# Gate stage of a streaming encoder: gating ahead of a slab's lo part, sigmoids behind copies, three sums and a row's split moved

## Chip, cores and metric

The kernel runs on one core of one Trainium2 chip. The metric is the device time of one execution in microseconds. Three runs of the kernel before gave 2480.63, 2480.68 and 2480.74; the median is 2480.68.

## What is computed

Two groups of frames (512 new ones and 8 streams of 16, 640 columns in all) pass through two layers that share their weights. A layer has a feed-forward half step, a mixer and a second feed-forward half step. The change is in the mixer. Cut to what matters here, the reference's mixer is:

```python
z = h @ w_in                                  # conv B, C, V, q, k, v and the gates g
g = sigmoid(g + b_gate)
g_conv, g_attn = split(g)                     # 1024 columns each
y_conv = B * causal_conv3(C * V)              # 512 channels
y_attn = band_attention(q, k, v)              # 512 channels
m = g_conv * (y_conv @ w_conv_out) + g_attn * (y_attn @ w_attn_out)
x = x + m @ w_o
```

## The kernel before

**Engines.** TensorE (PE in the profile, PEld for its weight loads) multiplies; VectorE (DVE) and ScalarE (ACT) do the elementwise work; SP and GpSimd (POOL) issue the loads of weights. In the gate stage TensorE, VectorE and ScalarE run their instructions in the order in which the code writes them (`ORDERED`), so an instruction that waits holds up all that stand behind it on its engine.

**Products.** Every fp32 operand is split in a hi part, cast by ScalarE, and a lo part, source minus hi, made by VectorE. A product is three matmuls: hi·hi, hi·lo and lo·hi. `prep` casts a slab's hi part (L361) and puts its lo part on a list; `flush` (L366) issues the lo parts of that list on VectorE. `split` (L233, L234) does the same for an operand of the next projection.

**By seven.** A two-by-two block product is made of seven block products instead of eight, named 11, 21, 22, N6, T5, T7 and T4. Their weights are blocks of the raw weights or sums of blocks. Each two raw slabs (`raw`, loaded by SP) give four slabs of weights: slab 0 for 11 and 21, slab 1 for N6 and T5, slab 2 for T7 and 22, slab 3 for T4 alone. Slab 1 is one sum `s` (L294) and a sum `one` that POOL's two accumulating loads have made a group ahead; slab 2 needs two more sums on VectorE. `following` preps the next slab but one, `ahead` makes the sums (and issues the loads) of the slab after that, `quiet` takes the slab that TensorE uses next.

**Gate stage.** The function `outputs` runs, in each of the two layers, gate pairs 2, 4, 6, 8, 10, 12 and 14 (two rows of 128 gates each, `gate_pair`) and four row groups of the two output projections (`rows`): co0 after pair 4 and co4 after pair 6 (y_conv, rows 0 to 3 and 4 to 7), ao0 after pair 10 and ao4 after pair 14 (y_attn). Each of them is seven blocks of twelve matmuls.

- A gate pair's blocks stand in the order 11, 21, N6, T5, T7, 22, T4. 11, N6, T7 and T4 add up in one accumulator `pa` (qa). T4 may start only when VectorE has read `pa` after T7 (L1563: g = pa + c5), since T4 adds on to it.
- A row group's blocks stand in the order 11, T5, N6, 21, T7, 22, T4 (`mul`, L1676). 11, N6, T7 and T4 add up in accumulator A (raco, raao), 21 is in B (rbco, rbao), T5 and 22 in c (rcco, rcao). ScalarE copies A after 11 (into B, or into s1 in group co0, L1692) and after N6 (into s2, rs_0, L1703); VectorE adds A after T7 to s5 (rs_1, L1716 through L294). T7 waits for the copy at L1703, T4 for the sum s5.
- `gated` multiplies a result into its gate (L1683, L1685): `gated(0, …, t1)` needs block 21, the others later blocks.

Small work is hung in by places: `call("s")`, "f", "a", "b", "c", "d" and "e" run what the caller gives for that place. `some` takes the next job of a list `tasks` (sigmoids, L1355, and ScalarE's copies of gates, L1736), `due` a result's last products, `total` adds an attention row to its conv row (`mm[m] += gates[8+m]`), `given` splits finished rows for the projection w_o. With the two rows of a tile side by side, rows 0 and 1 lie in `mm_0`, rows 2 and 3 in `mm_1`. The projection w_o (`po`) follows the stage; its second accumulator takes the place of the group's A.

Of the kernel before, what the change touches and what calls it, by code (L numbers as in the profile page):

```python
# [185 lines left out]
def two(ps):  # L186
    return ps[:, :, :HT]
# [7 lines left out]
def trunk(ctx: ExitStack, tc: tile.TileContext, xin, wst, small, pbias, samplebias, kcache, vcache, gfin,  # L195
# [24 lines left out]
    def acc(name):  # L220
        return banks["acc"].tile([P, 2, 512], F32, tag="acc", name=name)

    def att(name):
        return banks["att"].tile([P, 512], F32, tag="att", name=name)
# [4 lines left out]
    def tmp(name):  # L229
        return tp.tile([P, UW], F32, tag="t", name=name)[:, :T]  # L230
# [62 lines left out]
    def add(out, a, b, op=ALU.add):  # L293
        DVE.tensor_tensor(out=out, in0=a, in1=b, op=op)  # L294
# [69 lines left out]
    def flush(n=None):  # L364
        for lo, src, hi in pending[:n]:
            DVE.tensor_tensor(out=lo, in0=src, in1=hi.bitcast(F32), op=ALU.subtract)  # L366
        del pending[:n]
# [16 lines left out]
    def following(last_first=False):  # L384

        prep(len(ready), last_first)

    def ahead():

        source(len(ready))  # L390
# [5 lines left out]
    def quiet():  # L396

        used[0] += 1
        return ready[used[0] - 1]
# [83 lines left out]
    for k in range(KT):  # L483
# [4 lines left out]
        if k % 2 == 0:  # L488
            c = slice(k * P, (k + 2) * P)
# [1008 lines left out]
    def outputs(l, gp, X, st, cs, ycp, yas, sigmoid, gates):  # L1498


        rr, t1, t2 = st.rr, slice(0, HT), slice(HT, T)
# [28 lines left out]
        def gate_pair(m, at={}, rows_next=False):  # L1530
            n = f"{l}_{m}"
            pa, pb, pc = (att(f"q{i}{n}")[:, :HT] for i in "abc")

            def call(place):
                for f in at.get(place, ()):
                    f()

            s0 = quiet()
            ahead()
            call("s")  # L1540
            block(pa, s0, 0, X11, every, True, True)
            ACT.copy(c1, pa)
            following()
            call("f")
            flush()
            u, g = gates[m], gates[m + 1] = [mm[m + i] if m in (2, 6) else tmp(f"g{n}_{i}") for i in range(2)]
            block(pb, s0, 1, X21, every, True, True)
            add(u[:, t1], pb, c1)
            s1 = quiet()
            following()  # L1550
            flush()
            call("a")
            block(pa, s1, 0, XN6, every, False, True)
            ACT.copy(u2, pa)
            call("b")
            block(pc, s1, 1, XT5, every, True, True)
            ACT.copy(c5, pc)
            call("c")
            s2 = quiet()
            following()  # L1560
            ahead()
            block(pa, s2, 0, XT7, every, False, True)
            add(g[:, t2], pa, c5)  # L1563
            DVE.tensor_tensor(out=g[:, t2], in0=g[:, t2], in1=rr[:, t2], op=ALU.mult)
            flush()
            call("d")
            block(pc, s2, 1, X22, every, False, True)
            add(u[:, t2], pc, u2)
            s3 = quiet()
            following(rows_next)  # L1570
            if rows_next:
                flush(1)
            block(pa, s3, 0, XT4, every, False, True)
            DVE.tensor_tensor(out=g[:, t1], in0=pa, in1=rr[:, t1], op=ALU.mult)
            flush()
            off.append(lambda: DVE.tensor_tensor(out=u, in0=u, in1=rr, op=ALU.mult))
            tasks.extend((lambda: sigmoid(u, m), lambda: sigmoid(g, m + 1, -1.0)))
            call("e")
# [74 lines left out]
        def rows(y, ms, at={}, put_off=0):  # L1653

            n = f"{y.name}{l}_{ms[0]}"
            co = y.name == "co"
            gs = [gates[m + (0 if co else KT)] for m in ms]
            B, A = (acc(f"r{i}{n}") for i in "ba")
            a, b = ([z[:, u, :HT] for u in range(2)] for z in (A, B))
            c = [att(f"rc{n}_{u}")[:, :HT] for u in range(2)]  # L1660
            s1, s2, s5 = stage
            seed = seeded[0]
            seeded[0] = True

            def call(place):
                for f in at.get(place, ()):
                    f()

            def mul(ps, s, half, k, start):
                for u in range(2):  # L1670
                    for i in range(2):
                        kp = half * NP + 2 * u + i
                        wh, wl = (z[:, kp * P : (kp + 1) * P] for z in s)
                        xh, xl = y.kind(i, k)
                        for j, (w, x_) in enumerate(((wh, xh), (wh, xl), (wl, xh))):
                            PE.matmul(ps[u], w, x_, start=start and i == 0 and j == 0,  # L1676
                                      stop=i == 1 and j == 2, skip_group_check=True)

            def gated(r, src, t, scale=None):
                for u in range(2):  # L1680
                    g = gs[2 * r + u][:, t]
                    if scale is None:
                        DVE.tensor_tensor(out=g, in0=src[u], in1=g, op=ALU.mult)  # L1683
                    else:
                        DVE.scalar_tensor_tensor(out=g, in0=src[u], scalar=scale, in1=g,  # L1685
                                                 op0=ALU.mult, op1=ALU.mult)

            w = quiet()
            ahead()
            call("s")  # L1690
            mul(a, w, 0, "11", True)
            ACT.copy(two(B) if seed else s1, two(A))  # L1692
            following()
            call("f")
            flush()
            call("a")
            w1 = quiet()
            mul(c, w1, 1, "T5", True)
            for u in range(2):
                ACT.copy(s5[:, u], c[u])  # L1700
            call("b")
            mul(a, w1, 0, "N6", False)
            ACT.copy(s2, two(A))  # L1703
            call("c")
            mul(b, w, 1, "21", not seed)
            following()
            if not seed:
                add(s1, two(B), s1)
            flush()
            w = quiet()  # L1710
            following()
            gated(0, b if seed else [s1[:, u] for u in range(2)], t1)
            ahead()
            call("d")
            mul(a, w, 0, "T7", False)
            add(s5, two(A), s5)  # L1716
            flush()
            left = [lambda: gated(1, [s5[:, u] for u in range(2)], t2, -1.0),
                    lambda: gated(0, [s2[:, u] for u in range(2)], t2), lambda: gated(1, a, t1, -1.0)]

            if not put_off:
                left.pop(0)()
            mul(c, w, 1, "22", False)
            for u in range(2):
                add(s2[:, u], c[u], s2[:, u])
            w = quiet()
            following()
            if not put_off:
                left.pop(0)()
            mul(a, w, 0, "T4", False)  # L1730
            flush()
            while len(left) > put_off:
                left.pop(0)()
            off.extend(left)
            if co:
                tasks.extend(lambda u=u: ACT.copy(mm[ms[u]], gs[u]) for u in range(2))  # L1736
            call("e")
# [3 lines left out]
        def total(*ms):  # L1741
            for m in ms:
                add(mm[m], mm[m], gates[KT + m])

        def begun(*ms):
            for m in ms:
                mo[m] = tuple(hp.tile([P, T], F32R, tag=f"h{i}", name=f"m{l}_{m}{i}") for i in ("hi", "lo"))

        def given(*ms):
            for m in ms:  # L1750
                split(*mo[m], mm[m])

        def quarters(z):
            return z.rearrange("p c (a b) -> p (c a) b", a=2)

        def joined(*zs):
            return {k: [f for z in zs for f in z.get(k, ())] for k in "sfabcde"}

        due_, task = {"f": [due]}, lambda *ks: {k: [some()] for k in ks}
        yc = Mixed("co", [quarters(z) for z in ycp])  # L1760
        ya = Mixed("ao", [quarters(yas[:, 2 * i : 2 * i + 2]) for i in range(2)])
# [7 lines left out]
        gate_pair(8, joined(due_, one, task("b", "d")))  # L1769
        gate_pair(10, joined(due_, two_, task("b")), True)  # L1770
        rows(ya, (0, 1, 2, 3), joined(three, {"a": [due]}, task("b", "c", "d")), 1)
        gate_pair(12, joined({"f": [lambda: total(0)]}, {"a": [lambda: total(1)]}, {"a": [due]},
                             {"a": [lambda: total(2, 3)]}))
        gate_pair(14, joined(due_, task("b", "e"), {"c": [lambda: (begun(*range(4)), given(0, 2))]}), True)
        rows(ya, (4, 5, 6, 7), joined(due_, {"a": [lambda: given(1, 3)]}, task("b", "c")))
        assert not tasks
        begun(*range(4, KT))
        total(4, 5)
# [659 lines left out]
```

## Time and profile before

| | |
|---|---|
| median of three runs | 2480.68 us |
| the profiled execution | 2480.66 us |
| its span, first to last instruction | 2478.8 us |
| mean granted TensorE clock | 0.999 |
| TensorE matmul busy | 2461.0 us (99%) |
| VectorE busy | 2194.8 us (89%) |
| ScalarE busy | 1397.8 us (56%) |
| GpSimd busy | 326.0 us (13%) |
| gate stage of layer 0 | about 634 to 773.5 us from the span's start |
| gate stage of layer 1 | about 1863 to 2002 us |

A row of the timeline gives start and duration in microseconds, engine, line, operation, output and inputs (buffer numbers left out), shapes, a count of equal instructions that were drawn together, and in brackets the idle time of that engine before it with the instruction that ended it. A row of the waits view gives the waiting engine and line, what it waited for, the total, the number of times and the longest. A row of the windows gives the length of the stretch, then for PE, PEld, DVE, ACT and POOL the busy time and the number of instructions, then the granted clock, the share of the DMA engines and GB/s; its row "sum" adds up the stretches. Matmuls overlap: one starts before the one ahead of it has ended.

### The profile page before, as it was taken

Reading aid. Unit: us, or ns where it says so; the run is one execution under the profiler, and the core shown is the slowest. Engines: PE = TensorE matmul, PEld = TensorE weight load, DVE = VectorE, ACT = ScalarE, POOL = GpSimd, SP = SyncE. Lnnn points to the kernel's source line nnn. Section 1 sums busy time; section 2 is a strip of 40 time slices with the busy share of each in tenths; the row PEclk is TensorE's granted clock in tenths of the full one; section 3 lists DMA queues with packets and bytes.
Section 4 is the critical chain, followed back from the end, with each engine's and each line's share of the span. In section 5 each row is a group of like instructions: output and inputs, shape, how many; then the busy total and the mean of one; then the engine's idle time right before and its main releaser. Section 6 shows DMA issues by size and latency. Waiting matters only on the chain.

```text
span 2478.8 us, 44038 instructions
## 1 busy us (share of the span) xinstructions
PE 2461.0 (99%) x17216; PEld 2406.7 (97%) x17216; DVE 2194.8 (89%) x3684; ACT 1397.8 (56%) x2243; POOL 326.0 (13%) x491
## 2 busy tenths in 40 slices
PE   8999999999999999999999999999999999999999
PEld 8999999889999999999999999998899999999998
DVE  7999998888998899998799999988889979999997
ACT  6555555665655555555665555566656556555555
POOL 0211112211110001111001011121110000111111
PEclk9999999999999999999999999999999999999999
DMA  4443444335443334445334343453454333444444
GB/s 155 128 118 102 124 118 121 112 111 175 120 121 120 92 102 107 112 118 121 108 95 109 110 117 102 117 128 105 136 166 120 113 118 94 107 113 107 112 118 117
DMA packets 114417, 290.26 MB, mean 117 GB/s; under 512 B 13120, under 2 KB 52672, under 8 KB 114208
## 3 DMA queue, kind: packets, MB, share of 16 engines
q1 hardware_dynamic: 69552, 220.10, 27.6%
q0 software_dynamic: 44224, 67.09, 14.2%
q8 instruction: 135, 2.21, 0.4%
q14 instruction: 74, 0.61, 0.1%
q10 hardware_dynamic: 432, 0.25, 0.0%
HBM read 241.57 MB, written 7.94 MB: 101 GB/s over the span
## 4 chain that ended last, share of the span: by engine, by line
PE 90%; DVE 5%; ACT 2%; issue 1%; DMA 1%; SPq 0%; DVEq 0%; ACTq 0%; POOLq 0%
PE pab L460 12%; PE paa L460 11%; PE pcb L460 6%; PE daa L1148 6%; PE pca L460 5%; PE dab L1148 5%; PE po L436 5%; PE qa L460 3%; PE pbb L460 3%; PE dca L1148 3%; PE pba L460 3%; PE dcb L1148 2%; PE ma_cv L460 2%; PE ma_qk L460 2%; PE pv L1837 2%; PE qc L460 2%
## 5 line engine op out<-in xcount | busy, mean ns | idle before, releaser
L366 DVE TENSOR_TENSOR wlo<-raw,whi 128x512 fp32r<-128x512 f32 (+1 forms) x566 | 577.7, 1023 | 150.3 <-ACT whi L361 147.1
L361 ACT CAST whi<-raw 128x512 fp32r<-128x512 f32 (+1 forms) x566 | 500.6, 891 | 372.6 <-PE pbb L460 47.3
L361 ACT CAST whi<-s 128x1024 fp32r<-128x1024 f32 (+1 forms) x166 | 155.2, 935 | 288.9 <-issue 111.2
L460 PE MATMUL pab<-xhib,whi 128*128 128x320 f32 x704 | 217.7, 309 | 0.0
L460 PE MATMUL pab<-xlob,whi 128*128 128x320 f32 x704 | 217.2, 309 | 0.0
L460 PE MATMUL pab<-xhib,wlo 128*128 128x320 f32 x704 | 217.2, 309 | 0.0
L460 PE MATMUL paa<-xhia,whi 128*128 128x320 f32 x640 | 197.8, 309 | 0.2 <-DVE ga L294 0.2
L460 PE MATMUL paa<-xhia,wlo 128*128 128x320 f32 x640 | 197.5, 309 | 0.0
L460 PE MATMUL paa<-xloa,whi 128*128 128x320 f32 x640 | 197.5, 309 | 0.0
L366 DVE TENSOR_TENSOR wlo<-s,whi 128x1024 fp32r<-128x1024 f32 (+1 forms) x166 | 179.1, 1079 | 4.0 <-ACT whi L361 4.0
L1170 POOL DMA_DIRECT2D x<-c_a x80 | 69.8, 1018 | 574.8 <-ACT ahia L1052 205.6
L1170 POOL DMA_DIRECT2D x<-c_b x72 | 63.1, 1014 | 583.1 <-ACT ahib L1052 205.9
L460 PEld LDWEIGHTS pab<-xhib,whi 128*128 128x128 f32 x704 | 132.2, 188 | 0.9 <-issue 0.9
L460 PEld LDWEIGHTS pab<-xlob,whi 128*128 128x128 f32 x704 | 132.2, 188 | 0.0
L460 PEld LDWEIGHTS pab<-xhib,wlo 128*128 128x128 f32 x704 | 132.2, 188 | 0.0
L460 PEld LDWEIGHTS paa<-xhia,whi 128*128 128x128 f32 x640 | 120.1, 188 | 1.1 <-DVE ga L294 0.5
L460 PEld LDWEIGHTS paa<-xloa,whi 128*128 128x128 f32 x640 | 120.1, 188 | 0.2 <-DVE xloa L704 0.2
L460 PEld LDWEIGHTS paa<-xhia,wlo 128*128 128x128 f32 x640 | 120.1, 188 | 0.1
L294 DVE TENSOR_TENSOR raw<-s,raw 128x512 f32<-128x512 f32 x166 | 113.6, 684 | 0.0
L460 PE MATMUL pcb<-xhib,wlo 128*128 128x320 f32 x352 | 108.8, 309 | 0.0
L460 PE MATMUL pcb<-xhib,whi 128*128 128x320 f32 x352 | 108.7, 309 | 0.0
L460 PE MATMUL pcb<-xlob,whi 128*128 128x320 f32 x352 | 108.6, 309 | 0.0
(889 smaller groups left out, 8244.2 us busy)
## 6 DMA issues: line engine op xcount, KB each, us to landing
raw<-in_wst SPq DMA_DIRECT2D x375, 512.0 KB, 3.6
x<-c_a POOLq DMA_DIRECT2D x80, 160.0 KB, 4.5
x<-c_b POOLq DMA_DIRECT2D x72, 160.0 KB, 3.5
one<-in_wst POOLq DMA_DIRECT2D x40, 256.0 KB, 3.5
lent<-in_wst POOLq DMA_DIRECT2D x36, 256.0 KB, 3.8
kc<-in_kcache SPq DMA_DIRECT2D x32, 256.0 KB, 5.0
vc<-in_vcache SPq DMA_DIRECT2D x16, 512.0 KB, 4.5
x<-u_a POOLq DMA_DIRECT2D x40, 160.0 KB, 4.1
```

Of the source, the lines that this page charges most:

```text
L294: DVE.tensor_tensor(out=out, in0=a, in1=b, op=op)
L361: ACT.copy(hi[:, d], src[:, c])
L366: DVE.tensor_tensor(out=lo, in0=src, in1=hi.bitcast(F32), op=ALU.subtract)
L436: PE.matmul(ps[:, a, :HT], w, x[a] if isinstance(x, tuple) else x[:, a * HT : (a + 1) * HT], start=first and j == 0 and not seeded, stop=l ...
L460: PE.matmul(ps, a, b, start=start and kp == 0 and j == 0, stop=stop and kp == NP - 1 and j == 2, skip_group_check=True)
L1148: PE.matmul(ps[u], w, y, start=start and i == 0 and j == 0, stop=i == 1 and j == 2, skip_group_check=True)
L1170: POOL.dma_start(x[ms[2 * u + r]][:, cols], z[:, u], accum_op=ALU.add)
L1837: PE.matmul(pv[t], xx[:, t * P : (t + 1) * P], w[:, kk * AW : (kk + 1) * AW], start=c == 0 and kk == 0 and j == 0, stop=c == KT // 2 - 1 a ...
```

## The change

Nothing is added to the computation or taken from it; every engine has as many instructions as before. In `rows`, three moves:

- place "c", where a sigmoid of the task list is issued on ScalarE, goes from ahead of block 21 to behind the cast of slab 3;
- the first gating, `gated(0, …, t1)`, goes ahead of the flush of slab 3's lo part;
- `ahead()`, the sum `s` of the next group with the loads that belong to it, goes behind the sum s5;

On ScalarE, the copy after N6, the cast of slab 3, the sigmoid of place "c", the cast of the next slab and the sigmoid of place "d" now follow each other.

In the list of the groups: the totals of rows 0 and 1 now stand together at place "f" of pair 12 (before: 0 at "f", 1 at "a"); row 2's stays at "a"; row 3's goes to place "a" of pair 14. Row 2's split goes from place "c" of pair 14, where row 0's stays, to place "d", behind the lo part of the next slab. In group ao4 the two sigmoids go from places "b" and "c" to "c" and "d".

```diff
             ACT.copy(s2, two(A))
-            call("c")
             mul(b, w, 1, "21", not seed)
             following()
             if not seed:
                 add(s1, two(B), s1)
+            call("c")
+            gated(0, b if seed else [s1[:, u] for u in range(2)], t1)
             flush()
             w = quiet()
             following()
-            gated(0, b if seed else [s1[:, u] for u in range(2)], t1)
-            ahead()
             call("d")
             mul(a, w, 0, "T7", False)
             add(s5, two(A), s5)
+            ahead()
             flush()
...
-        gate_pair(12, joined({"f": [lambda: total(0)]}, {"a": [lambda: total(1)]}, {"a": [due]},
-                             {"a": [lambda: total(2, 3)]}))
-        gate_pair(14, joined(due_, task("b", "e"), {"c": [lambda: (begun(*range(4)), given(0, 2))]}), True)
-        rows(ya, (4, 5, 6, 7), joined(due_, {"a": [lambda: given(1, 3)]}, task("b", "c")))
+        gate_pair(12, joined({"f": [lambda: total(0, 1)], "a": [due, lambda: total(2)]}))
+        gate_pair(14, joined(due_, {"a": [lambda: total(3)]}, task("b", "e"),
+                             {"c": [lambda: (begun(*range(4)), given(0))], "d": [lambda: given(2)]}), True)
+        rows(ya, (4, 5, 6, 7), joined(due_, {"a": [lambda: given(1, 3)]}, task("c", "d")))
```

## Prediction

> **What bounds the kernel now.** I read the page's head, then TensorE's waits, then the windows of the first layer's gate stage (eight windows, 634.0 to 773.5 us), then the timeline around each wait.
>
> ```profile
> span 2478.8 us, 44038 instructions
> PE 2461.0 (99%) x17216; PEld 2406.7 (97%) x17216; DVE 2194.8 (89%) x3684; ACT 1397.8 (56%) x2243; POOL 326.0 (13%) x491
> ```
> ```profile
> PE raao L1676 <- DVE rs L294: 1.5, 2, 0.8
> ```
> ```profile
> sum 139.50, PE 137.43 PEld 135.96 DVE 127.30 ACT 83.89 POOL 11.42; mean PE 17.18 PEld 17.00 DVE 15.91 ACT 10.49 POOL 1.43
> ```
>
> TensorE is the bound, so an edit counts only by the waits of TensorE that it ends or makes. The waits view has each wait twice, once per layer; I work out one layer and double it. In these windows weight loading stood idle for 139.50 - 135.96 = 3.54 us. The timeline shows where:
>
> ```profile
> 670.01 0.19 PEld L1676 LDWEIGHTS raco<-y4co_0hi,whi 128*128 128x128 f32 x1 [0.46 <-issue]
> ...
> 707.12 0.19 PEld L460 LDWEIGHTS qa<-thi,whi 128*128 128x128 f32 x1 [0.18 <-DVE g L294]
> ...
> 728.33 0.31 PE L1676 MATMUL raao<-y4ao_0hi,whi 128*128 128x320 f32 x1
> ...
> 731.71 0.31 PE L1676 MATMUL rcao<-y2ao_1hi,wlo 128*128 128x320 f32 x1
> ...
> 732.74 0.19 PEld L1676 LDWEIGHTS raao<-y4ao_0hi,whi 128*128 128x128 f32 x1 [0.99 <-ACT whi L361]
> ...
> 732.77 0.39 PE L1676 MATMUL raao<-y4ao_0hi,whi 128*128 128x320 f32 x1 [0.75 <-DVE rs L294]
> ...
> 733.00 0.30 PE L1676 MATMUL raao<-y4ao_0lo,whi 128*128 128x320 f32 x1
> ...
> 746.03 0.19 PEld L460 LDWEIGHTS qa<-thi,whi 128*128 128x128 f32 x1 [0.98 <-DVE g L294]
> ...
> 758.84 0.19 PEld L460 LDWEIGHTS qa<-thi,whi 128*128 128x128 f32 x1 [0.49 <-DVE g L294]
> ...
> 768.05 0.19 PEld L1676 LDWEIGHTS raao<-y4ao_0hi,whi 128*128 128x128 f32 x1 [0.41 <-ACT rs L1703]
> ...
> 777.08 0.30 PEld L436 LDWEIGHTS po<-m_0hi,whi 128*128 128x128 f32 x2 [0.19 <-issue]
> ```
>
> These are, in order: block T4 of group co0, T4 of gate pair 8, T4 of group ao0, T4 of pairs 12 and 14, T7 of group ao4, and the projection's second accumulator. Matmuls follow each other at 0.147 us (728.33 to 731.71 is 23 steps), so a block of twelve takes 1.76. What a wait costs: 731.71 to 733.00 is 1.29 for two steps of 0.147, so 1.00 is lost. That is the weight load's idle time (0.99), not the matmul's 0.75.
>
> [...]
>
> **Row groups: gating ahead of the lo part.** VectorE's queue in group ao0 (g_8 are gates, wlo_8361/8362 the fourth slab's lo part, s_108 a slab sum, rs_1 the sum s5, rbao block 21):
>
> ```order
> -L366 TENSOR_TENSOR wlo_8362<-raw_8237,whi_8361 128x512
>  L1683 TENSOR_TENSOR g_8_0_8041<-rbao_0_8292,g_8_0_8041 128x320
>  L1683 TENSOR_TENSOR g_8_1_8042<-rbao_0_8292,g_8_1_8042 128x320
> -L294 TENSOR_TENSOR s_108_8377<-one_8239,raw_8365 128x512
> +L366 TENSOR_TENSOR wlo_8361<-raw_8237,whi_8360 128x512
>  L294 TENSOR_TENSOR rs_1_7304<-raao_0_8293,rs_1_7304 128x640
> -L366 TENSOR_TENSOR wlo_8368<-raw_8365,whi_8367 128x1024
> +L294 TENSOR_TENSOR s_108_8391<-one_8239,raw_8367 128x512
> +L366 TENSOR_TENSOR wlo_8370<-raw_8367,whi_8369 128x1024
> ```
> The gatings pass the lo part, and the s5 sum, which frees the accumulator for T4, passes the slab sum.
>
> ```profile
> 728.43 0.83 ACT L1355 ACTIVATE g<-g,sm 128x640 f32<-128x640 f32 x1 [0.96 <-DVE g L1576]
> ...
> 729.80 0.69 DVE L366 TENSOR_TENSOR wlo<-raw,whi 128x512 fp32r<-128x512 f32 x1 [1.41 <-ACT whi L361]
> ...
> 731.21 0.68 DVE L294 TENSOR_TENSOR s<-one,raw 128x512 f32<-128x512 f32 x1
> 731.81 0.82 DVE L294 TENSOR_TENSOR rs<-raao,rs 128x640 f32<-128x640 f32 x1
> ```
>
> Ao0: VectorE idled 1.41 for a cast that stood behind the sigmoid of 728.43. Now the cast goes first, and the gatings start when block 21 ends: 728.33 + 0.17 (a matmul lasts 0.31, 0.17 beyond the next one's start) = 728.5. Two gatings take 0.80 and the lo part 0.60 (the row groups' spacing), so VectorE is free at 729.9 and the sum waits only for T7's end, 728.33 + 1.76 + 0.17 = 730.26. It ends at 731.12 instead of 732.63; the load follows 0.11 later (732.63 to 732.74), and was due at 731.75. **0.99 goes**, margin about 0.5.
>
> ```profile
> 665.99 0.31 PE L1676 MATMUL rbco<-y2co_1hi,wlo 128*128 128x320 f32 x1
> ...
> 666.33 0.82 DVE L294 TENSOR_TENSOR capsm<-rbco,capsm 128x640 f32<-128x640 f32 x1
> ...
> 667.68 0.89 DVE L1683 TENSOR_TENSOR g<-capsm,g 128x320 f32<-128x320 f32 x2
> ...
> 669.08 0.82 DVE L294 TENSOR_TENSOR rs<-raco,rs 128x640 f32<-128x640 f32 x1
> ```
>
> Co0: the first add starts 0.03 after block 21's end (666.30), so TensorE's release is prompt. The slab sum (0.60) leaves the way; the gatings now read the add directly, at its end (667.15 + 0.04) where the lo part could start at 667.08: 0.11 back. The sum comes 0.49 earlier. **0.46 goes**, with no margin left.
>
> ```profile
> 692.84 0.31 PE L1676 MATMUL raco<-y4co_1hi,wlo 128*128 128x320 f32 x1
> ...
> 693.63 0.82 DVE L294 TENSOR_TENSOR rs<-raco,rs 128x640 f32<-128x640 f32 x1
> 694.37 1.22 DVE L366 TENSOR_TENSOR wlo<-raw,whi 128x1024 fp32r<-128x1024 f32 x1
> ...
> 706.59 0.48 DVE L294 TENSOR_TENSOR g<-qa,c 128x320 f32<-128x320 f32 x1
> ```
> ```profile
> 698.20:721.20 23.00, 23.00 (x158) 22.82 (x157) 22.83 (x42) 14.48 (x25) 2.54 (x4) 1.00 0.48 138
> ```
>
> Co4, a cost: no wait stood here. T7 ends at 693.15; the slab sum used the time before it, and now follows. Sum at 693.20, slab sum 693.94, next lo part 694.54 instead of 694.37. From there VectorE (third count of the window, 22.83 of 23.00) has no gap to absorb it until the add of 706.59, for which pair 8's T4 waits already: 0.18 becomes 0.35. **0.17 is added.**
>
> The moved step also issues loads, on SP and on POOL:
>
> ```profile
> one<-in_wst POOLq DMA_DIRECT2D x40, 256.0 KB, 3.5
> ```
>
> Both queues keep their order. Two such loads, 7 us, fill one of two buffers, whose use is a group (7 × 1.76 = 12.3 us) further on: nothing. If that cover failed, the slab sum would wait by the difference.
>
> **Gate pair 12.** VectorE's queue (mm += g are the totals):
>
> ```order
>  L294 TENSOR_TENSOR mm_0_7301<-mm_0_7301,g_8_0_8041 128x640
> -L366 TENSOR_TENSOR wlo_8449<-raw_8365,whi_8448 128x1024
> -L294 TENSOR_TENSOR g_12_0_8453<-qb_12_8431,capsm_4819 128x320
> -L366 TENSOR_TENSOR wlo_8469<-raw_8372,whi_8468 128x512
>  L294 TENSOR_TENSOR mm_0_7301<-mm_0_7301,g_8_1_8042 128x640
> +L366 TENSOR_TENSOR wlo_8449<-raw_8367,whi_8448 128x1024
> +L294 TENSOR_TENSOR g_12_0_8454<-qb_12_8431,capsm_4819 128x320
> +L366 TENSOR_TENSOR wlo_8470<-raw_8386,whi_8469 128x512
>  L1685 SCALAR_TENSOR_TENSOR g_10_0_8177<-raao_0_8293,g_10_0_8177 128x320
>  L1685 SCALAR_TENSOR_TENSOR g_10_1_8178<-raao_0_8293,g_10_1_8178 128x320
>  L294 TENSOR_TENSOR mm_1_7302<-mm_1_7302,g_10_0_8177 128x640
> +L294 TENSOR_TENSOR s_110_8512<-one_8388,raw_8502 128x512
> ```
> The second total moves ahead of the lo part, and the fourth leaves for pair 14.
>
> ```profile
> 739.74 1.23 DVE L366 TENSOR_TENSOR wlo<-raw,whi 128x1024 fp32r<-128x1024 f32 x1 [0.44 <-ACT whi L361]
> ...
> 743.42 1.55 DVE L294 TENSOR_TENSOR mm<-mm,g 128x640 f32<-128x640 f32 x2
> 744.89 0.69 DVE L294 TENSOR_TENSOR s<-one,raw 128x512 f32<-128x512 f32 x1
> 745.49 0.49 DVE L294 TENSOR_TENSOR g<-qa,c 128x320 f32<-128x320 f32 x1
> ```
>
> A total takes 0.74 (743.42 to 744.89 for two). VectorE enters the pair 0.91 earlier (the sum 1.51 earlier, the slab sum's 0.60 back). The second total costs 0.74 - 0.44 of idle = 0.30 there, and two totals leave further on: 745.49 becomes 745.49 - 0.91 + 0.30 - 1.48 = 743.40, ending at 743.89. TensorE comes 0.99 earlier and wants T4's weights at 745.05 - 0.99 = 744.06. **0.98 goes**, margin 0.1 to 0.2.
>
> **Gate pair 14.**
>
> ```profile
> 756.22 0.83 DVE L234 TENSOR_TENSOR m_0lo<-mm,m_0hi 128x640 fp32r<-128x640 f32 x1 [1.82 <-ACT m_0hi L233]
> ...
> 758.30 0.48 DVE L294 TENSOR_TENSOR g<-qa,c 128x320 f32<-128x320 f32 x1
> ```
>
> The fourth total fits into the 1.82 of idle time. Row 2's lo part (0.74, as the total) leaves the way of the add at 758.30: **0.49 goes**, margin 0.25.
>
> **Group ao4.** ScalarE's queue (rs_0 is the copy s2, g_14 the sigmoids):
>
> ```order
>  L1700 COPY rs_1_7304<-rcao_4_1_8703 128x320
> -L1355 ACTIVATE g_14_0_8585<-g_14_0_8585,sm 128x640
>  L1703 COPY rs_0_7303<-raao_4_8701 128x640
> -L1355 ACTIVATE g_14_1_8586<-g_14_1_8586,sm 128x640
> -L361 CAST whi_8769<-raw_8648 128x512
> -L361 CAST whi_8775<-raw_8773 128x1024
> -L361 CAST whi_8812<-raw_8780 128x1024
> +L361 CAST whi_8767<-raw_8646 128x512
> +L1355 ACTIVATE g_14_0_8584<-g_14_0_8584,sm 128x640
> +L361 CAST whi_8776<-raw_8774 128x1024
> +L1355 ACTIVATE g_14_1_8585<-g_14_1_8585,sm 128x640
> ```
> The sigmoid ahead of the copy goes behind it and a cast.
>
> ```profile
> 766.58 0.84 ACT L1355 ACTIVATE g<-g,sm 128x640 f32<-128x640 f32 x1
> 767.32 0.68 ACT L1703 COPY rs<-raao 128x640 f32<-128x640 f32 x1
> ...
> 769.27 0.69 DVE L366 TENSOR_TENSOR wlo<-raw,whi 128x512 fp32r<-128x512 f32 x1 [1.75 <-ACT whi L361]
> ```
>
> The copy comes 0.74 earlier (766.58 to 767.32). But its chain hangs on VectorE, which does row 2's lo part ahead of it, so it does not gain pair 14's 0.49: 0.41 - 0.74 + 0.49 = 0.16 stays, **0.25 goes**. The gatings' 0.80 moves into the 1.75 of idle time, so **0.19** goes at the projection.
>
> **Sum.** 0.99 + 0.46 - 0.17 + 0.98 + 0.49 + 0.25 + 0.19 = 3.19 per layer, 6.4 in all. The profiled execution took 2480.66 us (span 2478.8), as the median of 2480.68: 2474.3, with a span of 2472.4. The granted clock is 1.00 in the quoted window (third number from the end): no term.
>
> **Rivals.** Forecast, 2474.3: 0.74. Its own range: if pair 8's wait does not grow and goes too (0.35) and T7's rest goes (0.16), 3.7 per layer, 2473.3; if the three small margins fail by 0.1 and pair 8's by 0.2, 0.5 back, 2475.3.
>
> *VectorE 0.3 later than counted throughout*: back come 0.3 (co0), 0.3 (pair 8), 0.15 (pair 12), 0.05 (pair 14), 0.25 (T7): 2.1 left, 2476.4. For it: zero margin at co0, and 127.30 of 139.50 us busy. Against: the idle times above. 0.14.
>
> *Waits cost only the matmul's idle time*: then 0.24 less comes back at each of the four T4 waits that go (0.99 against 0.75), 2.2 left, 2476.2; 0.04. Against: the 1.29 measured. [...]
>
> *The moved waits only meet the next one*, since VectorE has the same work: 2480.7. Against: the same idle times. 0.04.
>
> *Slower*: the gatings, now first in VectorE's strict order, wait not for block 21 but for T7's end, 1.76 later, with lo part, sums and slab sum queued behind. Then the sum starts 0.42 (co0) and 0.97 (co4) later than before; TensorE loses 0.42 and, with 0.05 of slack (sum and release end at 694.56, the load is due at 692.84 + 12 × 0.147 = 694.60), 0.92; pair 8's T4 0.65 more; ao0 and pair 12 gain only 0.24; pair 14, ao4 and the projection keep 0.93: 0.8 per layer worse, 2482.3. Linear between, the gain is gone from 1.4 us after block 21 on. Against: co0's add, 0.03 after its release. 0.04.
>
> A measurement can tell about 0.2% (5.0 us) from no change. Faster by more means below 2475.7: the forecast, less what falls beyond its range, and a little of the first rival: 0.74. The slower rival stays within 0.2%, so slower by more is 0.02, and same 0.24. The range, 2473.2 to 2476.6, leaves out the last two rivals and some 0.06 of the forecast's ends.
>
> **What would show it.** Right: no idle time on weight loads at T4 of co0, ao0, pairs 12 and 14; 0.3 to 0.4 at pair 8; at most 0.2 at ao4's T7; the ao0 gating within 0.1 of block 21's end. Wrong: weight-load idle time in the stage above 1.5 us per layer, a wait on a lo part, or a slab sum waiting for a load.

## The result, and the profile after

The changed kernel takes 2474.33 us, the median of 11 runs (2473.73 to 2476.59), where the kernel before took 2480.68 in 11 runs beside it (2480.34 to 2481.27). The ratio is 0.9975, with a 95% interval of 0.9966 to 0.9984: 6.35 us less, 0.25%, and the interval leaves out 1. The forecast was 2474.3. The profiled execution took 2474.65 us.

The head of the page of the changed kernel:

```profile
span 2472.9 us, 44032 instructions
PE 2459.8 (99%) x17216; PEld 2408.0 (97%) x17216; DVE 2194.5 (89%) x3684; ACT 1397.2 (57%) x2243; POOL 326.7 (13%) x491
```

The busy times of all engines are within 1.5 us of those before, so no work went. What went is idle time of TensorE. First, the sum of eight windows over the first layer's gate stage (634.0 to 771.0 us) and the weight loads' waits on a sum `g` by the waits view; then, from the weight loads' timeline, the two rows of this stage that still have an idle time (707.33 and 765.55), and among those that have none now T4 of co0, ao0 and pair 12 and the projection's second accumulator:

```profile
sum 137.00, PE 136.93 PEld 136.47 DVE 128.39 ACT 84.17 POOL 11.45; mean PE 17.12 PEld 17.06 DVE 16.05 ACT 10.52 POOL 1.43
```
```profile
PEld qa L460 <- DVE g L294: 0.7, 2, 0.3
```
```profile
670.06 0.19 PEld L1676 LDWEIGHTS raco<-y4co_0hi,whi 128*128 128x128 f32 x1
...
707.33 0.19 PEld L460 LDWEIGHTS qa<-thi,whi 128*128 128x128 f32 x1 [0.34 <-DVE g L294]
...
731.92 0.19 PEld L1676 LDWEIGHTS raao<-y4ao_0hi,whi 128*128 128x128 f32 x1
...
744.22 0.19 PEld L460 LDWEIGHTS qa<-thi,whi 128*128 128x128 f32 x1
...
765.55 0.19 PEld L1676 LDWEIGHTS raao<-y4ao_0hi,whi 128*128 128x128 f32 x1 [0.19 <-ACT rs L1703]
...
774.30 0.34 PEld L436 LDWEIGHTS po<-m_0hi,whi 128*128 128x128 f32 x2
```

Weight loading stood idle for 137.00 - 136.47 = 0.53 us, at T4 of pair 8 and at T7 of group ao4. Before, the seven waits that the prediction lists summed to 0.46 + 0.18 + 0.99 + 0.98 + 0.49 + 0.41 + 0.19 = 3.70. So 3.17 went per layer; the second layer's rows read the same (0.34 and 0.19), which makes 6.34 in both.

The stage's length agrees. The first matmul of pair 2 and the first of the projection, in TensorE's timeline of the kernel before and then of the changed one:

```profile
634.49 0.31 PE L460 MATMUL qa<-hhim,whi 128*128 128x320 f32 x1
...
773.47 0.45 PE L436 MATMUL po<-m_0hi,whi 128*128 128x320 f32 x2
```
```profile
635.01 0.31 PE L460 MATMUL qa<-hhim,whi 128*128 128x320 f32 x1
...
770.93 0.45 PE L436 MATMUL po<-m_0hi,whi 128*128 128x320 f32 x2
```

From 138.98 to 135.92 us, 3.06 less, and the projection's wait on top. This execution came to the stage 0.52 later than the other, in work that the change does not touch, so the two profiled spans differ by only 5.9.

VectorE's timeline of the changed kernel, at the places where the prediction worked out a time: group ao0, then group co0, then group co4 with the add in pair 8, and the add in pair 12.

```profile
728.74 0.89 DVE L1683 TENSOR_TENSOR g<-rbao,g 128x320 f32<-128x320 f32 x2
729.55 0.68 DVE L366 TENSOR_TENSOR wlo<-raw,whi 128x512 fp32r<-128x512 f32 x1
730.50 0.82 DVE L294 TENSOR_TENSOR rs<-raao,rs 128x640 f32<-128x640 f32 x1 [0.27 <-PE raao L1676]
```
```profile
667.71 0.89 DVE L1683 TENSOR_TENSOR g<-capsm,g 128x320 f32<-128x320 f32 x2
668.52 0.68 DVE L366 TENSOR_TENSOR wlo<-raw,whi 128x512 fp32r<-128x512 f32 x1
669.13 0.82 DVE L294 TENSOR_TENSOR rs<-raco,rs 128x640 f32<-128x640 f32 x1
```
```profile
693.23 0.82 DVE L294 TENSOR_TENSOR rs<-raco,rs 128x640 f32<-128x640 f32 x1 [0.27 <-PE raco L1676]
693.98 0.68 DVE L294 TENSOR_TENSOR s<-one,raw 128x512 f32<-128x512 f32 x1
694.58 1.22 DVE L366 TENSOR_TENSOR wlo<-raw,whi 128x1024 fp32r<-128x1024 f32 x1
...
706.80 0.48 DVE L294 TENSOR_TENSOR g<-qa,c 128x320 f32<-128x320 f32 x1
...
743.53 0.48 DVE L294 TENSOR_TENSOR g<-qa,c 128x320 f32<-128x320 f32 x1
```

In ao0 the 1.41 of idle time before the lo part is gone: the lo part follows the gatings, and the sum waits for T7's end, as worked out. In co0 nothing waits any more, but the sum starts at the moment at which VectorE comes free. In co4 the sum waits for T7's end (0.27) and the slab sum follows it, ahead of the lo part: the order that was to cost 0.17 at pair 8. In pair 12 the add ends at 743.53 + 0.48 = 744.01, 0.21 ahead of T4's weight load at 744.22; 743.89 and 744.06, 0.17 apart, were worked out.

In pair 14 VectorE's idle time before row 0's split is 1.08 where it was 1.82: the fourth total fills 0.74 of it.

```profile
752.53 0.82 DVE L294 TENSOR_TENSOR mm<-mm,g 128x640 f32<-128x640 f32 x1
...
754.43 0.83 DVE L234 TENSOR_TENSOR m_0lo<-mm,m_0hi 128x640 fp32r<-128x640 f32 x1 [1.08 <-ACT m_0hi L233]
```

### The profile page after: what moved, and what is told of

Its sections match the earlier page's. It is cut to its first block, busy times and chain, and to the rows that moved or that the text cites. A ratio compares the mean times of both kernels' runs of the same rounds, so it can differ in the third digit from the quotient of the medians.

```text
span 2472.9 us, 44032 instructions
## 1 busy us (share of the span) xinstructions
PE 2459.8 (99%) x17216; PEld 2408.0 (97%) x17216; DVE 2194.5 (89%) x3684; ACT 1397.2 (57%) x2243; POOL 326.7 (13%) x491
## 4 chain that ended last, share of the span: by engine, by line
PE 94%; DVE 3%; ACT 2%; issue 1%; DMA 0%; DVEq 0%; ACTq 0%; POOLq 0%
PE pab L460 12%; PE paa L460 11%; PE pcb L460 6%; PE daa L1148 6%; PE pca L460 5%; PE dab L1148 5%; PE po L436 5%; PE qa L460 4%; PE pbb L460 3%; PE dca L1148 3%; PE pba L460 3%; PE dcb L1148 2%; PE ma_cv L460 2%; PE ma_qk L460 2%; PE pv L1837 2%; PE qc L460 2%
```

## The experiments

Each kernel was run beside the kernel before, which gave medians of 2480.88, 2480.71 and 2481.14 us on the three chips used. All compute the whole reference. Diffs are against the changed kernel; `...` stands for lines that are not shown.

**The row groups alone, and the lists alone.** The first keeps the three moves in `rows` and has the lists of jobs as before; the second is the reverse.

```diff
rows_only:
-        gate_pair(12, joined({"f": [lambda: total(0, 1)], "a": [due, lambda: total(2)]}))
+        gate_pair(12, joined({"f": [lambda: total(0)]}, {"a": [lambda: total(1)]}, {"a": [due]},
+                             {"a": [lambda: total(2, 3)]}))
...
lists_only:
+            call("c")
             mul(b, w, 1, "21", not seed)
...
-            call("c")
-            gated(0, b if seed else [s1[:, u] for u in range(2)], t1)
             flush()
             w = quiet()
             following()
+            gated(0, b if seed else [s1[:, u] for u in range(2)], t1)
+            ahead()
             call("d")
             mul(a, w, 0, "T7", False)
             add(s5, two(A), s5)
-            ahead()
```

> Only the three moves inside the row groups; the totals, row 2's split and group ao4's sigmoids stand as before. My theory (TensorE waits for single instructions of VectorE and ScalarE, and the waits add up one by one): weight loads idle per layer 0 at T4 of co0 and ao0, 0.35 us at pair 8's T4, 1.06 at pair 12's T4 (0.98 plus the 0.08 by which TensorE comes earlier than VectorE), 0.49 at pair 14's T4, 0.41 at ao4's T7, together 2.3 against 3.7 before: 2477.9 us. Rival (the row groups' waits only move on to the pairs, since VectorE has the same work): pair 12 takes back the whole 0.99 and the time stays within 0.5 us of 2480.7.

> Only the moves of the totals, of row 2's split and of ao4's sigmoids; the code inside the row groups stands as before. My theory: the waits of co0 (0.46), pair 8 (0.18) and ao0 (0.99) stay, those of pairs 12 and 14 and of the projection go, 0.16 to 0.2 stays at ao4's T7, together 1.8 per layer: 2476.9 us. Rival (the parts need each other): pair 12 keeps 0.5 or more of its wait without the row group's earlier sum, 2478 or more.

rows_only took 2477.91 us (2477.63 to 2478.98), ratio 0.9988 (0.9979 to 0.9997). The weight loads of its first gate stage:

```profile
706.72 0.19 PEld L460 LDWEIGHTS qa<-thi,whi 128*128 128x128 f32 x1 [0.34 <-DVE g L294]
...
744.72 0.19 PEld L460 LDWEIGHTS qa<-thi,whi 128*128 128x128 f32 x1 [1.07 <-DVE g L294]
...
757.52 0.19 PEld L460 LDWEIGHTS qa<-thi,whi 128*128 128x128 f32 x1 [0.49 <-DVE g L294]
...
766.73 0.19 PEld L1676 LDWEIGHTS raao<-y4ao_0hi,whi 128*128 128x128 f32 x1 [0.40 <-ACT rs L1703]
```

The waits at co0 and ao0 are gone. Pair 12's is 1.07 where it was 0.98, 0.09 more as expected, and pair 14's stays at 0.49, instead of growing by the 0.99 that went at ao0. The rival by which the waits only move on falls here.

lists_only took 2477.80 us (2476.94 to 2478.98), ratio 0.9987 (0.9978 to 0.9995), 0.9 above what was expected. Its weight loads:

```profile
646.01 0.19 PEld L460 LDWEIGHTS qa<-thi,whi 128*128 128x128 f32 x1 [0.25 <-DVE mm L294]
671.11 0.19 PEld L1676 LDWEIGHTS raco<-y4co_0hi,whi 128*128 128x128 f32 x1 [0.46 <-issue]
708.22 0.19 PEld L460 LDWEIGHTS qa<-thi,whi 128*128 128x128 f32 x1 [0.18 <-DVE g L294]
733.83 0.19 PEld L1676 LDWEIGHTS raao<-y4ao_0hi,whi 128*128 128x128 f32 x1 [0.99 <-ACT whi L361]
767.43 0.19 PEld L1676 LDWEIGHTS raao<-y4ao_0hi,whi 128*128 128x128 f32 x1 [0.19 <-ACT rs L1703]
776.46 0.30 PEld L436 LDWEIGHTS po<-m_0hi,whi 128*128 128x128 f32 x2 [0.20 <-issue]
```

Pairs 12 and 14 wait no more, ao4's T7 waits 0.19 instead of 0.41, and co0, pair 8 and ao0 wait as before: the two halves of the change act each at its own places. Of the 0.9 too much, 0.4 is the projection's wait, which I had expected to go with the lists (0.20 in each of two layers); it goes by the moves inside `rows`, made in ao4 too, which this kernel lacks. The first row, at T4 of pair 2, is new and lies ahead of everything that the change touches; it is taken up at the end.

**Which move in the row groups takes ao0's wait.** Three kernels put back the sigmoid's move, the gatings' move, or both; the slab sum stays behind s5 in all.

```diff
sigmoid_back:
             ACT.copy(s2, two(A))
+            call("c")
...
-            call("c")
             gated(0, b if seed else [s1[:, u] for u in range(2)], t1)
...
gating_back:
             call("c")
-            gated(0, b if seed else [s1[:, u] for u in range(2)], t1)
             flush()
             w = quiet()
             following()
+            gated(0, b if seed else [s1[:, u] for u in range(2)], t1)
```

> The changed kernel with place c, the sigmoid, back ahead of block 21, so that the sigmoid stands ahead of slab 3's cast again. My theory: with the gatings ahead of the lo part VectorE has work until the cast comes, the lo part in ao0 ends at most 0.5 us later and the sum s5 waits for T7's end all the same: no wait comes back, 2474.3 us. Rival (the sigmoid behind the copy is what ended ao0's wait): 0.4 us or more of weight-load idle time at ao0's T4, 2475.1 to 2476.3 us.

> The changed kernel with the first gating back behind slab 3's lo part. My theory: the cast now comes ahead of the sigmoid, so that the lo part is done while VectorE would wait for block 21, and the sum s5 starts at T7's end as in the changed kernel: no wait comes back, and co0's margin grows by 0.1: 2474.3 us. Rival (the gating's place is what ended ao0's wait): 0.4 us or more at ao0's T4, 2475.1 to 2476.3 us.

> The changed kernel with both the sigmoid and the gating back in their old places; of the moves inside the row groups only the slab sum's stays. My theory (either of the two moves ends ao0's wait, and without both it stands again, less the slab sum's 0.60): per layer 0.44 us of weight-load idle time at ao0's T4, and 0.41 at pair 12's T4, since VectorE enters the pair as late as before; 0.34 at pair 8 and 0.19 at ao4's T7 as in the changed kernel: 2476.0 us. Rival (the slab sum's move alone did it): 2474.3 us.

sigmoid_back took 2474.17 us (2474.02 to 2474.72) and gating_back 2474.22 (2473.92 to 2475.05), both at a ratio of 0.9972 (0.9961 to 0.9983): no different from the changed kernel. Their weight loads wait 0.35 at pair 8 and 0.20 at ao4's T7, and nowhere else. both_back took 2476.53 us (2475.77 to 2477.20), ratio 0.9982 (0.9974 to 0.9991). Its VectorE in group ao0, its weight loads there and in pair 12, and the matmul of the first of these two loads:

```profile
730.30 0.69 DVE L366 TENSOR_TENSOR wlo<-raw,whi 128x512 fp32r<-128x512 f32 x1 [1.41 <-ACT whi L361]
730.91 0.88 DVE L1683 TENSOR_TENSOR g<-rbao,g 128x320 f32<-128x320 f32 x2
731.71 0.81 DVE L294 TENSOR_TENSOR rs<-raao,rs 128x640 f32<-128x640 f32 x1
```
```profile
732.64 0.19 PEld L1676 LDWEIGHTS raao<-y4ao_0hi,whi 128*128 128x128 f32 x1 [0.39 <-issue]
...
745.26 0.19 PEld L460 LDWEIGHTS qa<-thi,whi 128*128 128x128 f32 x1 [0.29 <-DVE g L294]
```
```profile
732.67 0.39 PE L1676 MATMUL raao<-y4ao_0hi,whi 128*128 128x320 f32 x1 [0.15 <-DVE rs L294]
```

With both put back, the 1.41 of idle time for a cast that stands behind a sigmoid is there again, and 0.39 of ao0's 0.99 (0.44 was expected); the other 0.60 is the slab sum, which still stands behind s5. VectorE enters pair 12 late enough for 0.29 (0.41 was expected), and the projection waits 0.20 again, which was not expected. The median lies 0.5 above the 2476.0 that was. So, with the slab sum behind s5, the rest of ao0's wait goes by either of two moves: put the cast ahead of the sigmoid, or give VectorE the gatings to do in its place. One is redundant beside the other, but not both.

**The slab sum, the row's split, the fourth total: each put back alone.**

```diff
sum_back:
+            ahead()
             call("d")
             mul(a, w, 0, "T7", False)
             add(s5, two(A), s5)
-            ahead()
...
split_back:
-                             {"c": [lambda: (begun(*range(4)), given(0))], "d": [lambda: given(2)]}), True)
+                             {"c": [lambda: (begun(*range(4)), given(0, 2))]}), True)
...
total_back:
-        gate_pair(12, joined({"f": [lambda: total(0, 1)], "a": [due, lambda: total(2)]}))
-        gate_pair(14, joined(due_, {"a": [lambda: total(3)]}, task("b", "e"),
+        gate_pair(12, joined({"f": [lambda: total(0, 1)], "a": [due, lambda: total(2, 3)]}))
+        gate_pair(14, joined(due_, task("b", "e"),
```

> The changed kernel with the slab sum back ahead of the sum s5. My theory: co0's T4 waits again, 0.57 to 0.62 us; ao0's does not, because its sum s5 still ends before the block; pair 8's T4 no longer waits, because the slab sum runs in the time before T7's end: per layer 0.60 back and 0.34 gone, 2474.8 us. Rival (pair 8's wait has another cause than the slab sum): it stays at 0.34, 2475.5 us.

> The changed kernel with row 2's split back beside row 0's in pair 14. My theory: pair 14's T4 waits again, 0.5 us, and ao4's T7 no longer does, since the lo part no longer stands ahead of the slab sums on which ScalarE's copy hangs: per layer 0.52 back and 0.19 gone, 2475.0 us. Rival (T7's rest has another cause): 0.19 stays, 2475.4 us.

> The changed kernel with the fourth total back in pair 12. My theory: pair 12's T4 waits 0.74 less its margin of 0.15, 0.6 us per layer, and nothing else changes: 2475.5 us. Rival (the earlier sum in ao0 alone ended pair 12's wait): no wait, 2474.3 us.

sum_back took 2474.99 us (2474.33 to 2477.34), ratio 0.9977 (0.9968 to 0.9986). VectorE and the weight load at group co0:

```profile
667.83 0.69 DVE L366 TENSOR_TENSOR wlo<-raw,whi 128x512 fp32r<-128x512 f32 x1
668.43 0.69 DVE L294 TENSOR_TENSOR s<-one,raw 128x512 f32<-128x512 f32 x1
669.03 0.82 DVE L294 TENSOR_TENSOR rs<-raco,rs 128x640 f32<-128x640 f32 x1
```
```profile
669.97 0.19 PEld L1676 LDWEIGHTS raco<-y4co_0hi,whi 128*128 128x128 f32 x1 [0.59 <-issue]
```

The slab sum ahead of s5 costs one slab sum (0.60) at co0, and pair 8 does not wait at all: the move is worth 0.59 in one group and costs 0.34 behind another. At ao0 nothing waits here: with the sigmoid and the gatings moved, the slab sum's move is not needed there.

split_back took 2474.74 us (2474.14 to 2475.52), ratio 0.9975 (0.9965 to 0.9984). Pair 14 waits 0.49 again and ao4's T7 not at all, as expected. total_back took 2475.46 us (2475.05 to 2477.55), ratio 0.9979 (0.9970 to 0.9988). Pair 12 waits 0.54 (0.6 was expected). The weight loads of split_back at pair 14 and of total_back at pair 12:

```profile
756.71 0.19 PEld L460 LDWEIGHTS qa<-thi,whi 128*128 128x128 f32 x1 [0.49 <-DVE g L294]
```
```profile
744.79 0.19 PEld L460 LDWEIGHTS qa<-thi,whi 128*128 128x128 f32 x1 [0.54 <-DVE g L294]
```

**No wait left.** The last two waits answer to two of these moves, so both can go: the slab sum stays ahead of s5 in the groups other than co0, and row 2's split is taken apart, its cast at place "d" of pair 14 as in the changed kernel (`high`), its lo part at the head of group ao4's place "a" (`low`). The definitions of these two are not shown. `seed` is false in group co0 and true in the other groups. The changed kernel was run again beside it.

```diff
             following()
+            if seed:
+                ahead()
             call("d")
             mul(a, w, 0, "T7", False)
             add(s5, two(A), s5)
-            ahead()
+            if not seed:
+                ahead()
...
-                             {"c": [lambda: (begun(*range(4)), given(0))], "d": [lambda: given(2)]}), True)
-        rows(ya, (4, 5, 6, 7), joined(due_, {"a": [lambda: given(1, 3)]}, task("c", "d")))
+                             {"c": [lambda: (begun(*range(4)), given(0))], "d": [lambda: high(2)]}), True)
+        rows(ya, (4, 5, 6, 7), joined(due_, {"a": [lambda: (low(2), given(1, 3))]}, task("c", "d")))
```

> The changed kernel with two more moves, against the two waits that are left: in all row groups but co0 the slab sum goes back ahead of the sum s5 (against pair 8's 0.34 us), and row 2's lo part goes from pair 14 to place a of group ao4, behind the slab sums, while its cast stays (against 0.19 at ao4's T7). My theory: no weight load of the gate stage waits, 0.53 us less per layer: 1.06 us under the changed kernel, 2473.3 us. Rival (the lo parts in ao4 now come too late for its T4 or the slab sum delays T4 of co4 or ao0): a new wait of 0.2 us or more there, no gain.

> The changed kernel once more, beside the version with no waits on the same chip: 2474.3 us within 0.5, with 0.34 us at pair 8's T4 and 0.19 at ao4's T7 in each layer.

no_waits took 2473.18 us (2472.84 to 2473.33), ratio 0.9969 (0.9956 to 0.9981): the lowest median of all. The changed kernel took 2474.87 beside it (2474.07 to 2475.84), ratio 0.9974 (0.9964 to 0.9984). no_waits is 1.7 lower on that chip, and 1.15 lower than the changed kernel's first median; 2 × 0.53 = 1.06 was expected, and after_again lies 0.07 above the range expected of it. The two profiled spans differ by 1.8 (2473.1 and 2471.3). Of this, 1.07 is the changed kernel's waits (0.54 and 0.53); the rest was there before the stage, to which it came at 635.22 us and no_waits at 634.50. Its two gate stages, by windows from 634 and 1861 us (each of 137 us; PE, PEld, DVE, ACT and POOL busy):

```profile
634.00:771.00 137.00, 137.00 (x937) 137.00 (x936) 128.81 (x220) 83.91 (x136) 11.46 (x16) 1.00 0.40 119
1861.00:1998.00 137.00, 137.00 (x937) 137.00 (x937) 128.89 (x219) 82.46 (x134) 12.07 (x17) 1.00 0.41 121
```

TensorE and its weight loads are busy in all 137.00 of 137.00, and the projection's loads behind them wait for nothing either: in this stage no wait is left that another order could take away.

All runs together, with the weight loads' idle time at the places of the change (us, first layer, the projection's wait included, the waits of the last section left out) and the median less twice that:

| kernel | idle per layer | median | median less 2 × idle |
|---|---|---|---|
| before | 3.70 | 2480.68 | 2473.3 |
| rows_only | 2.30 | 2477.91 | 2473.3 |
| lists_only | 2.02 | 2477.80 | 2473.8 |
| both_back | 1.42 | 2476.53 | 2473.7 |
| total_back | 1.08 | 2475.46 | 2473.3 |
| split_back | 0.83 | 2474.74 | 2473.1 |
| sum_back | 0.78 | 2474.99 | 2473.4 |
| sigmoid_back | 0.55 | 2474.17 | 2473.1 |
| gating_back | 0.55 | 2474.22 | 2473.1 |
| after_again | 0.54 | 2474.87 | 2473.8 |
| the change | 0.53 | 2474.33 | 2473.3 |
| no_waits | 0 | 2473.18 | 2473.2 |

The last column stays within 0.7 us while the idle time goes from 3.70 to 0: one count, the weight loads' idle time, accounts for every kernel to that. The kernels from split_back down differ by less, and their medians alone do not rank them.

The profiles narrow it, since they give the stage's own length. The first matmul of pair 2 and of the projection in no_waits:

```profile
634.50 0.31 PE L460 MATMUL qa<-hhim,whi 128*128 128x320 f32 x1
...
769.89 0.45 PE L436 MATMUL po<-m_0hi,whi 128*128 128x320 f32 x2
```

That is 135.39 us, where the kernel before had 138.98, rows_only 137.91 and the changed kernel 135.92. In all 24 stages (twelve profiles, two layers) the length less the weight loads' idle time between these two matmuls, all waits counted, lies between 135.39 and 135.64; the length less the matmuls' idle time lies between 135.39 and 137.05. So in these stages the weight loads' idle time is the price of a wait, and the matmuls' is not.

## Why the prediction was right

**The bound and the price of a wait.** The whole forecast hangs on the weight load's idle time as the price. It forecast 3.19 per layer; 3.17 was measured, and 6.35 between the medians. The rival by which only the matmul's idle time counts would have given 2476.2. That is 1.9 above the median, but within the interval of its ratio (0.9984 of 2480.68 is 2476.7); the length of the stage, above, is what rules it out.

The loads at the waits speak against it too. In both_back the load at 732.64 starts 0.03 before its matmul, after 0.39 of idle time where the matmul has 0.15, so its weights were not loaded ahead while the matmul waited. Where nothing waits, a load does start further ahead of its matmul. In pair 12 of the changed kernel the load at 744.22 starts 0.14 before its matmul, while the matmul before it (744.21 and 0.31) runs:

```profile
744.21 0.31 PE L460 MATMUL qc<-hhim,wlo 128*128 128x320 f32 x1
744.36 0.31 PE L460 MATMUL qa<-thi,whi 128*128 128x320 f32 x1
```

What holds a load back at a wait is not shown.

**Group ao0 (0.99 forecast, 0.99 gone).** Right in time and margin. The gating starts at 728.74, 0.04 after block 21's end (its last matmul: 728.39 and 0.31), the sum ends at 731.32 and the load starts at 731.92, so about 0.5 is left. But the change does more for it than is needed, as sigmoid_back, gating_back and sum_back show: any one of its three moves can be taken back without a wait at ao0. The prediction counted the cast, the gatings and the slab sum in one sum and did not say so.

**Group co0 (0.46, 0.46).** Right, with no margin, as said: the sum ends at 669.95 and the load starts 0.11 later, at 670.06, the very delay from sum to load that the prediction read at ao0. Of the steps in it, the slab sum's 0.60 is shown by sum_back (0.59).

**Co4 and pair 8 (a cost of 0.17, measured 0.16).** Right as a net. sum_back takes it apart: with the sigmoid and the gatings moved and the slab sum not, pair 8 does not wait, so these two moves took away the 0.18 that stood here before, and the slab sum's move put 0.34 in its place. no_waits has no wait there either, with co0's wait gone too. Which of the two moves it is was not separated; the prediction took the 0.18 as given.

**Pair 12 (0.98, 0.98) and pair 14 (0.49, 0.49).** Right. The margin at pair 12 is 0.16, within the 0.1 to 0.2 forecast: of the 0.21 from the add to the load, the load needs 0.05, as at pair 8, where the add ends at 707.28 and the load that waits for it starts at 707.33. rows_only shows that the lists are needed for both, total_back that the fourth total's leaving is needed for pair 12, split_back that row 2's split was all of pair 14's wait.

**Group ao4 (0.25 forecast, 0.22 gone) and the projection (0.19, 0.19).** 0.19 is left at T7 where 0.16 was forecast. That it hangs on where row 2's lo part stands is shown by split_back and no_waits, which put it elsewhere and have no wait there. The prediction put the projection's wait down to the gatings' move; the sigmoid's does as well: it came back in lists_only and both_back, which lack both, and not in sigmoid_back or gating_back.

**The slower rival** asked for gatings that wait until T7's end. They started 0.04 after block 21 in ao0, so its condition did not hold. **VectorE 0.3 later than counted** did not come either: the waits are within 0.03 of their forecasts.

## What to carry to other kernels

When one engine is busy for 99% of the span, list its idle times place by place and ask for each which instruction frees it and what stands ahead of that instruction in its engine's order without need; work that has a later reader goes behind it, and the sum of the idle times removed is the gain, to within 0.7 us in these medians. Read them in the weight loads' row: of the 0.34 at pair 8 the matmuls' row shows 0.07 (the matmul at 707.33 starts that long after the end of the one before it, 706.95 and 0.31), and its timeline gives no idle time there. A move made for several places at once should be priced at each: the slab sum's was worth 0.59 in one group and cost 0.34 after another, and making it a choice by group gave both. Where two moves remove the same wait, undo them one at a time and then together, or each looks worthless.

## What was not expected

In some executions the gate stage had a wait at its entry, ahead of everything that the change touches: 0.25 and 0.28 at T4 of pair 2 in lists_only, 0.28 there and 0.29 at the stage's first block in both_back, 0.28 and 0.69 in total_back's second layer. Neither the kernel before nor the changed one had it in its profile. These profiled executions (2478.98, 2476.93 and 2476.86 us) lie 1.2, 0.4 and 1.4 above their kernels' medians; those waits (0.53, 0.57 and 0.97 in all) cover only a part of the first and third. Another part can lie ahead of the stage: the twelve profiled executions come to it between 634.22 and 635.32 us, lists_only last. All this fits the spread of the changed kernel's own runs, up to 2.3 us above its median, but what delays the attention stage's last results in such an execution was not settled, nor whether it is the kernels' order or chance.
